# A hybrid two-layer model on one Trainium2 core: the first norm laid out in one order, other credits and costs for the background of the expert loops, and gate rows turned ahead of the last gates

## The chip, the cores and the metric

The kernel runs on one core of one Trainium2 chip. The metric is the device time of one execution in microseconds (us), and of several runs the median counts. All the matrix work goes through TensorE (PE in the profile); VectorE (DVE), ScalarE (ACT) and GpSimd (POOL) do the rest, each in the order in which its instructions were put, and SyncE (SP), ScalarE and GpSimd issue the DMA transfers.

## The reference

A sequence of 512 tokens with 1024 features goes through two layers. Each layer has a mixer and an expert network, each behind a norm whose shift, scale and gate come from one conditioning vector `c`:

```python
for layer in range(DEPTH):
    g, mw, mb = mix_norms[layer]
    shift, scale, gate = ada_modulation(c, mw, mb)      # silu(c) @ mw + mb, in three parts
    h = rms_norm(x, g) * (1.0 + scale) + shift
    mixer = rglru_mixer if layer % N_MIXERS == 0 else fox_mixer
    x = x + gate * mixer(h, *mixer_params[layer])
    g, mw, mb = ffn_norms[layer]
    shift, scale, gate = ada_modulation(c, mw, mb)
    h = rms_norm(x, g) * (1.0 + scale) + shift
    x = x + gate * peer_ffn(h, *peer_params[layer])
```

Layer 0 mixes by a gated linear recurrence (two input projections, a causal convolution of width 4, block-diagonal gates, a scan, gelu), layer 1 by attention with forget gates. The expert network picks for each token and each of 8 heads the 16 best of 16384 experts by two sets of keys, and adds up `gate * gelu(u . h) * v` over the 128 picks of a token.

## The kernel before

**Numbers.** Products are taken in three passes: every float32 operand is split into a rounded high part (`hi`, a copy on ScalarE) and the remainder (`lo`, a subtraction on DVE), and a product is hi·hi + hi·lo + lo·hi. So each weight block costs ScalarE a `whi` (L179) and DVE a `wlo` (L180) ahead of TensorE. `Stream` holds the plan of all weight blocks of the whole kernel in order; `fetch` issues a load on SP's queue, `fill` splits, `take` hands a block out.

**Order.** The program is written as straight Python and a list scheduler with a model of the machine lays out each engine's instructions. It may move an instruction ahead of another one that stands earlier in the program, unless both are given to `tc.keep_in_program_order` (here `pin`): pinned instructions of an engine keep the program's order among themselves. Within an engine the chip then executes strictly in the order laid out.

**The first norm** (`norm_first`, L252 to L348) is woven with the first modulation and the first four projections. The modulation columns of layer 0's mixer are dot products on DVE (`dot`, L300) of weight rows with silu(c); ScalarE makes a column of each (L302, L305). The token tiles are squared and scaled (L364 to L370), transposed into eight PSUM banks (L311), and for each of the eight feature blocks k `finish(k)` makes `hk` (L327), `hhi` (L328) and `hlo` (L329). Blocks of the first projection's weights are taken one step behind, and `products(k - 1)` runs the matmuls that are possible by then (L321 to L323). Of this only the dots and the `hlo` are pinned.

**The recurrent mixer** (`lru`) then takes chunk after chunk: projection, convolution, a second projection through gelu (L701), and behind each second chunk the gates of two chunks (L660 to L680). `Background` runs the modulation rows of what follows: `pump(credit)` adds credit and runs steps of generators as long as it is positive; each step yields its cost. `grow_fn` (`row_of`, L224) turns the eight gate columns into a row: a transpose on TensorE, a copy on ScalarE (L231), a small store on ScalarE's queue (L232) and a broadcast load on GpSimd's (L233). It stands between the last two groups of gates; the out-projection (L528 to L530) follows.

**The expert loop** (`peer`, L1147 and around) treats 384 of the 512 tokens densely: it goes over 128 chunks of 128 experts; a chunk's activations are either computed (24 matmuls, L486 to L488) or, for 56 of them, loaded back from where an earlier stage stored them (`at<-ascr`); they are multiplied by the gates (L1133), split (L1137, L1140) and multiplied with the chunk's `v` (18 matmuls, L1147). The last 128 tokens are done beside it by gathering rows of single experts (`gathered`, L1023 to L1064): 128 steps with `u` rows (L1044), then modulation rows (`mod_gen`, L196 to L221: a load on GpSimd's queue and a DVE product, L211), then 128 steps with `v` rows (L1059 for the first, L1061), then in layer 0 six more modulation rows. All use a ring of 8 buffers. Each step is put at 1.2 of credit, and `PUMPS` says how much credit a computed and a stored chunk give. What is left when the loop ends is run behind it by `bg.finish()`. Then the ring's room is given back, the tokens `x` are loaded into it by GpSimd (L123), and for each token tile from the last to the first DVE adds the gated result (L498, L499), ScalarE squares (L381), and DVE scales (L398) for the next norm, whose transposes (L425) follow on TensorE.

**The attention mixer** (`fox`) ends with the same `grow_fn`, behind its last output gates (L1367, L1368), ahead of `finish_mixer`, which splits `y` (`split`, L248 and L249) for the out-projection.

## Time and profile before

| what | us |
|---|---|
| median of 3 runs | 3088.3 (3087.58 to 3090.57) |
| the profiled execution, device time | 3089.21 |
| its span, first to last instruction | 3087.4 |
| granted TensorE clock, mean | 0.996 |

The profile shows one execution. In the rows of the timeline the columns are: start in us from the span's start, duration in us, engine (a `q` behind it marks the issue of a DMA), line of the kernel, operation, output<-inputs by the program's names, shapes, count of merged instructions, and in brackets the idle time of the engine just before and what ended it. In the grouped rows of the page stand, behind the count, the busy time in us, the mean of one in ns, and after the second bar the idle time of the engine ahead of these instructions. A row of the waits says who waited for whom: total in us, times, longest. A row by windows gives for a stretch its length and each engine's busy time (instructions) in the order PE, weight loads, DVE, ACT, POOL, then the granted TensorE clock, the share of the DMA engines' time and GB/s. Matmuls overlap, so the distance of their starts tells their rate, not their duration.

### The profile page before, as it was taken

How to read it: one execution, taken by the hardware profiler on the slowest of the kernel's cores; microseconds unless marked ns; L12 is line 12 of the kernel's file. 1: busy time of each engine (PE TensorE's matmuls, PEld its weight loads, DVE VectorE, ACT ScalarE, POOL GpSimd, SP SyncE). 2: the span in 40 equal slices, each digit the busy share in tenths (PEclk: the TensorE clock that was granted, in tenths of full speed). 3: DMA queues.
4: the chain of work that ended last, by engine and by line, in shares of the span. 5: the costliest groups of instructions: out<-in, count | busy, mean ns of one | idle time of the engine just before them, and what ended most of it. 6: DMA issues, size and time to landing. Idle time of an engine off the chain costs nothing.

```text
span 3087.4 us, 44585 instructions
## 1 busy us (share of the span) xinstructions
PE 3026.6 (98%) x16196; PEld 2676.5 (87%) x16196; DVE 2569.5 (83%) x5272; ACT 1480.4 (48%) x2183; POOL 953.1 (31%) x842
## 2 busy tenths in 40 slices
PE   7999999999999999999899999999999999999999
PEld 5778899998888888888777778899998888888888
DVE  7876989878888988898679967899868887888887
ACT  5764247873333333333458844267853333333332
POOL 0001430006554335554011003400025454445452
PEclk9999999999999999999999999999999999999999
DMA  7443245779999999999432123346799999999996
GB/s 275 169 163 141 97 153 197 265 292 390 381 361 374 366 352 372 373 347 341 164 121 77 63 103 128 121 157 245 271 333 377 335 357 349 355 328 354 355 326 242
DMA packets 295469, 815.85 MB, mean 264 GB/s; under 512 B 24624, under 2 KB 147536, under 8 KB 266704
## 3 DMA queue, kind: packets, MB, share of 16 engines
q1 hardware_dynamic: 164304, 388.77, 35.1%
q0 software_dynamic: 89408, 321.43, 27.9%
q10 hardware_dynamic: 41536, 102.80, 8.7%
q8 instruction: 127, 2.08, 0.3%
q14 instruction: 94, 0.77, 0.1%
HBM read 731.89 MB, written 81.02 MB: 263 GB/s over the span
## 4 chain that ended last, share of the span: by engine, by line
PE 71%; DVE 15%; issue 6%; ACT 4%; DMA 3%; POOL 1%; SPq 0%; DVEq 0%; POOLq 0%; ACTq 0%
PE vacc L1147 29%; PE pacc L486 11%; PE pacc L488 10%; PE pacc L487 10%; PE gps L991 3%; DVE wlo L180 2%; DVE ge L898 1%; DMA at<-ascr 1%; DVE tk L823 1%; PE oacc L529 1%; PE oacc L528 1%; PE oacc L530 1%; DVE mw L211 1%; ACT whi L179 1%; DVE idxs L822 1%
## 5 line engine op out<-in xcount | busy, mean ns | idle before, releaser
L179 ACT ACTIVATE whi<-wraw 128x1024 fp32r<-128x1024 f32 (+1 forms) x646 | 665.3, 1034 | 581.5 <-PE pacc L487 401.2
L486 PE MATMUL pacc<-hhi,whi 128*128 128x384 f32 (+1 forms) x2600 | 915.7, 352 | 1.2 <-ACT ge L701 1.2
L488 PE MATMUL pacc<-hhi,wlo 128*128 128x384 f32 (+1 forms) x2600 | 909.4, 350 | 5.5 <-DVE wlo L180 5.2
L487 PE MATMUL pacc<-hlo,whi 128*128 128x384 f32 (+1 forms) x2600 | 907.3, 349 | 0.0
L180 DVE TENSOR_TENSOR wlo<-wraw,whi 128x1024 fp32r<-128x1024 f32 (+1 forms) x584 | 705.8, 1212 | 202.6 <-ACT whi L179 199.8
L1147 PE MATMUL vacc<-wlo,wh 128*128 128x512 f32 x1536 | 600.2, 391 | 1.8 <-DVE wlo L180 1.8
L1147 PE MATMUL vacc<-whi,wl 128*128 128x512 f32 x1536 | 600.4, 391 | 0.0
L1147 PE MATMUL vacc<-whi,wh 128*128 128x512 f32 x1536 | 597.8, 389 | 0.0
L488 PEld LDWEIGHTS pacc<-hhi,wlo 128*128 128x128 f32 x2600 | 488.8, 188 | 31.5 <-DVE wlo L180 8.5
L486 PEld LDWEIGHTS pacc<-hhi,whi 128*128 128x128 f32 x2600 | 489.3, 188 | 27.7 <-ACT ge L701 1.6
L487 PEld LDWEIGHTS pacc<-hlo,whi 128*128 128x128 f32 x2600 | 489.3, 188 | 26.9
L1137 ACT ACTIVATE wh<-at 128x384 fp32r<-128x384 f32 x256 | 133.9, 526 | 740.1 <-DVE at L1133 356.9
L1031 POOL DMA_INDIRECT rows<-in_l_v_dram,ei x256 | 362.8, 1417 | 368.5 <-DVE accg L1061 332.1
L1031 POOL DMA_INDIRECT rows<-in_l_u_dram,ei x256 | 370.8, 1448 | 323.4 <-DVE rows L1044 267.8
L1147 PEld LDWEIGHTS vacc<-whi,wl 128*128 128x128 f32 x1536 | 288.3, 188 | 60.3
L1147 PEld LDWEIGHTS vacc<-wlo,wh 128*128 128x128 f32 x1536 | 288.3, 188 | 59.6 <-DVE wlo L180 2.2
L1147 PEld LDWEIGHTS vacc<-whi,wh 128*128 128x128 f32 x1536 | 288.5, 188 | 57.1
L1061 DVE SCALAR_TENSOR_TENSOR accg<-rows,act,accg 128x1024 f32<-128x1024 f32 x254 | 325.2, 1280 | 2.6 <-DMA rows<-in_l_v_dram,ei 2.2
L1044 DVE SCALAR_TENSOR_TENSOR rows<-rows,hn 128x1024 f32<-128x1024 f32 x256 | 304.7, 1221 | 0.0
L1133 DVE TENSOR_TENSOR at<-at,gtile 128x384 f32<-128x384 f32 x256 | 141.6, 555 | 135.0 <-DMA at<-ascr 127.4
L993 ACT ACTIVATE st<-gps 128x512 f32<-128x512 f32 x192 | 186.4, 1115 | 28.9 <-PE gps L991 28.4
L180 POOL TENSOR_TENSOR wlo<-wraw,whi 128x1024 fp32r<-128x1024 f32 (+1 forms) x62 | 125.3, 2032 | 185.3 <-ACT whi L179 185.3
(314 smaller groups left out, 3421.8 us busy)
## 6 DMA issues: line engine op xcount, KB each, us to landing
wraw<-in_l_uT_dram SPq DMA_DIRECT2D x128, 1024.0 KB, 5.7
wraw<-in_l_v_dram SPq DMA_DIRECT2D x128, 1024.0 KB, 9.3
gscr<-st ACTq DMA_DIRECT2D x48, 1024.0 KB, 4.9
gtile<-gscr SPq DMA_DIRECT2D x90, 512.0 KB, 12.8
mw<-in_l_ffn_mw_dram POOLq DMA_DIRECT2D x48, 512.0 KB, 4.7
ascr<-at ACTq DMA_DIRECT2D x112, 192.0 KB, 3.1
at<-ascr ACTq DMA_DIRECT2D x112, 192.0 KB, 6.9
mw<-in_l_mix_mw_dram POOLq DMA_DIRECT2D x32, 512.0 KB, 6.9
```

Of the source, the lines that this page charges most:

```text
L179: self.pin(nc.scalar.activation(hi, raw, AF.Copy))
L180: self.pin((nc.gpsimd if self.on_pool else nc.vector).tensor_sub(lo, raw, hi))
L486: nc.tensor.matmul(ps, whi[:, k, :], hhi[:, k, :n], start=(k == 0), stop=False)
L487: nc.tensor.matmul(ps, whi[:, k, :], hlo[:, k, :n], start=False, stop=False)
L488: nc.tensor.matmul(ps, wlo[:, k, :], hhi[:, k, :n], start=False, stop=(k == KD - 1))
L993: A.activation(st[:, :, q * 4:q * 4 + 4].rearrange("p e t -> p t e"), gps, AF.Copy, scale=1.0 / GSCALE)
L1031: i = nc.gpsimd.indirect_dma_start(out=rows, out_offset=None, in_=src, in_offset=bass.IndirectOffsetOnAxis(ap=ei[:, j:j + 1], axis=0))
L1044: V.scalar_tensor_tensor(r, r, 1.0, hn, op0=OP.mult, op1=OP.mult, accum_out=act[:, j:j + 1]))
L1061: tc.keep_in_program_order(V.scalar_tensor_tensor(acc, r, w, acc, op0=OP.mult, op1=OP.add))
L1133: pin(V.tensor_tensor(at.rearrange("p (b t) -> p b t", t=16), at.rearrange("p (b t) -> p b t", t=16), gts[c // 8][:, :, c % 8, :], op=OP.m ...
L1137: pin(A.activation(wh, at, AF.Copy))
L1147: T.matmul(acc[t][d], x[:, ts], y[:, d, :], start=(i == 0 and x is wh and y is vh), stop=(i == PK - 1 and x is wl))
```

## The change

Five edits:

1. In `norm_first` every ScalarE and DVE instruction of the columns, of `finish` and of the weight splits is pinned. Weight block k is split in step k (not k + 1): `whi` right behind `hhi`, `wlo` behind `hlo`, through a list `hold` in which the stream leaves the subtraction. `products(k)` follows in the same step. Blocks 4 and 5 are split behind the last step.
2. Behind the first column stands a gelu of a single column (128x1) into a spare tile, so that gelu's table is loaded there.
3. `PUMPS` go from (4.15, 1.3) to (4.45, 1.4) in layer 0 and from (3.75, 1.15) to (3.9, 1.2) in layer 1, and a modulation row in the expert loops counts 1.45 instead of 1.2.
4. The gate row is turned earlier: in `lru` in chunk 9 of 0 to 10, ahead of the last two groups of gates; in `fox` ahead of the last three gates.
5. The first step with a `v` row (L1059) is pinned like the others.

```diff
-PUMPS = ((4.15, 1.3), (3.75, 1.15))
+PUMPS = ((4.45, 1.4), (3.9, 1.2))
...
             self.pin(nc.scalar.activation(hi, raw, AF.Copy))
-            self.pin((nc.gpsimd if self.on_pool else nc.vector).tensor_sub(lo, raw, hi))
+            if self.hold is None:
+                self.pin((nc.gpsimd if self.on_pool else nc.vector).tensor_sub(lo, raw, hi))
+            else:
+                self.hold.append((lo, raw, hi))
...
-        yield 1.2
+        yield unit
...
+        pin = tc.keep_in_program_order
+
         def dot(r):
...
             if r < KD:
-                A.activation(cols[r], d, AF.Identity, bias=sub.b[:, r:r + 1])
+                pin(A.activation(cols[r], d, AF.Identity, bias=sub.b[:, r:r + 1]))
...
         dot(KD)
+        pin(A.activation(g.spare[:, 0:1], g.mhalf, AF.Gelu))
         for t in g.order:
...
+        def high(b):
+            g.stream.spare, g.stream.hold, g.stream.pin = nw if b < 2 else None, hold, pin
+            w.append(g.stream.take(0))
+            g.stream.spare, g.stream.hold, g.stream.pin = None, None, lambda x: x
...
-            A.activation(hk, xt[k], AF.Identity, scale=cols[KD + k], bias=cols[k])
-            A.activation(hhi[:, k, :], hk, AF.Copy)
-            return lambda: tc.keep_in_program_order(V.tensor_sub(hlo[:, k, :], hk, hhi[:, k, :]))
+            pin(A.activation(hk, xt[k], AF.Identity, scale=cols[KD + k], bias=cols[k]))
+            pin(A.activation(hhi[:, k, :], hk, AF.Copy))
+            return lambda: pin(V.tensor_sub(hlo[:, k, :], hk, hhi[:, k, :]))
 
         for k in range(KD):
             if k in (0, 2):
                 next(moved)
             low = finish(k)
+            if k < m:
+                high(k)
             if k + 1 < KD:
                 dot(KD + k + 1)
                 dot(k + 1)
             low()
-            if 1 <= k <= m:
-                g.stream.spare = nw if k <= 2 else None
-                w.append(g.stream.take(0))
-            if k == KD - 2:
+            if k < m:
+                pin(V.tensor_sub(*hold.pop(0)))
+            if k == KD - 1:
                 g.stream.fill(m + 1)
-            if k:
-                products(k - 1)
-        products(KD - 1)
+            products(k)
...
                         gates((j - 2, j - 1))
+                    if j == NR - 2:
+                        grow = grow_fn(psum)
                     bg.pump(LP)
                 bg.finish()
-                grow = grow_fn(psum)
                 gates((NR - 1,))
...
                 if j == 0:
-                    V.tensor_scalar(acc, r, w, None, op0=OP.mult)
+                    i = V.tensor_scalar(acc, r, w, None, op0=OP.mult)
                 else:
-                    tc.keep_in_program_order(V.scalar_tensor_tensor(acc, r, w, acc, op0=OP.mult, op1=OP.add))
+                    i = V.scalar_tensor_tensor(acc, r, w, acc, op0=OP.mult, op1=OP.add)
+                tc.keep_in_program_order(i)
...
                         bg.finish()
+                        if j == KD - 1:
+                            grow = grow_fn(psum)
                         n = (KD - LATE) // 2
                         for i in range(LATE + (j + 2 - KD) * n, LATE + (j + 3 - KD) * n):
                             gate(i)
-                grow = grow_fn(psum)
...
-            return mod_gen(g, pool, a[p + "_mw"], mods[p], rows, bufs, bufs < 8, queue, ring)
+            return mod_gen(g, pool, a[p + "_mw"], mods[p], rows, bufs, bufs < 8, queue, ring, 1.45 if ring else 1.2)
```

More of the change, by code (lines that the diff above doesn't have):

```diff
@@ L152, in __init__ @@
         self.spare = None
+        self.hold = None
         self.pin = lambda x: x
@@ L193, in take, with mod_gen @@
         return got
-def mod_gen(g, pool, mwT, sub, rows, bufs=2, pin=True, queue=None, ring=None):
+def mod_gen(g, pool, mwT, sub, rows, bufs=2, pin=True, queue=None, ring=None, unit=1.2):
     nc = g.nc
@@ L298, in dot @@
             d = nw.tile([128, 1], F32, name="dot", tag="dot", bufs=4)
-            tc.keep_in_program_order(
-                V.scalar_tensor_tensor(wf, wf, 1.0, g.sc, op0=OP.mult, op1=OP.mult, accum_out=d))
+            pin(V.scalar_tensor_tensor(wf, wf, 1.0, g.sc, op0=OP.mult, op1=OP.mult, accum_out=d))
             if r < KD:
-                A.activation(cols[r], d, AF.Identity, bias=sub.b[:, r:r + 1])
+                pin(A.activation(cols[r], d, AF.Identity, bias=sub.b[:, r:r + 1]))
             else:
                 k = r - KD
-                A.activation(cols[r], d, AF.Identity, scale=sub.g[:, k:k + 1], bias=bg[:, k:k + 1])
+                pin(A.activation(cols[r], d, AF.Identity, scale=sub.g[:, k:k + 1], bias=bg[:, k:k + 1]))
         dot(KD)
+        pin(A.activation(g.spare[:, 0:1], g.mhalf, AF.Gelu))
         for t in g.order:
@@ L313, in norm_first @@
                 dot(0)
-        w, ps = [], []
+        w, ps, hold = [], [], []
+        def high(b):
+            g.stream.spare, g.stream.hold, g.stream.pin = nw if b < 2 else None, hold, pin
+            w.append(g.stream.take(0))
+            g.stream.spare, g.stream.hold, g.stream.pin = None, None, lambda x: x
         def products(s):
```

## The prediction

> **What bounds the kernel now.** The page comes first, then TensorE's waits, then the timeline around each place where TensorE stands.
>
> ```profile
> span 3087.4 us, 44585 instructions
> ...
> PE 3026.6 (98%) x16196; PEld 2676.5 (87%) x16196; DVE 2569.5 (83%) x5272; ACT 1480.4 (48%) x2183; POOL 953.1 (31%) x842
> ...
> L179 ACT ACTIVATE whi<-wraw 128x1024 fp32r<-128x1024 f32 (+1 forms) x646 | 665.3, 1034 | 581.5 <-PE pacc L487 401.2
> ...
> L1061 DVE SCALAR_TENSOR_TENSOR accg<-rows,act,accg 128x1024 f32<-128x1024 f32 x254 | 325.2, 1280 | 2.6 <-DMA rows<-in_l_v_dram,ei 2.2
> L1044 DVE SCALAR_TENSOR_TENSOR rows<-rows,hn 128x1024 f32<-128x1024 f32 x256 | 304.7, 1221 | 0.0
> ```
>
> TensorE is busy for 3026.6 of 3087.4 us and the change takes no matmul away, so all it can win is 60.8 us of TensorE's idle time and whatever matmuls lose at a lower clock. No saving on another engine counts unless it ends in one of those gaps. Of TensorE's waits (total, times, longest) these belong to the change, beside the start's:
>
> ```profile
> PE pacc L488 <- DVE wlo L180: 5.2, 6, 2.0
> ...
> PE pacc L486 <- ACT ge L701: 1.2, 1, 1.2
> ...
> PE oacc L528 <- ACT grow L231: 0.9, 1, 0.9
> ```
>
> TensorE stands, or runs at a lower clock, at four places where the diff works: the first norm (11 to 56 us), the step from u rows to v rows in layer 0's expert loop (1122), the end of that loop (1489 to 1519), and the places where the gate row is turned (206, 1806). The last 100 us hold no gap that the change can reach: there TensorE works without a stop into the last adds.
>
> **The first norm.** The vector engine's timeline:
>
> ```profile
> 18.74 1.21 DVE L300 SCALAR_TENSOR_TENSOR mrow<-mrow,sc 128x1024 f32<-128x1024 f32 x1
> ...
> 23.87 1.23 DVE L180 TENSOR_TENSOR wlo<-wraw,whi 128x1024 fp32r<-128x1024 f32 x1 [2.17 <-ACT whi L179]
> 25.02 1.22 DVE L300 SCALAR_TENSOR_TENSOR mrow<-mrow,sc 128x1024 f32<-128x1024 f32 x1
> ...
> 27.31 0.69 DVE L329 TENSOR_TENSOR hlo<-hk,hhi 128x512 fp32r<-128x512 f32 x1
> 27.91 1.22 DVE L300 SCALAR_TENSOR_TENSOR mrow<-mrow,sc 128x1024 f32<-128x1024 f32 x1
> ...
> 29.05 1.22 DVE L180 TENSOR_TENSOR wlo<-wraw,whi 128x1024 fp32r<-128x1024 f32 x1
> ...
> 45.64 1.23 DVE L300 SCALAR_TENSOR_TENSOR mrow<-mrow,sc 128x1024 f32<-128x1024 f32 x1
> ...
> 49.66 2.36 DVE L180 TENSOR_TENSOR wlo<-wraw,whi 128x1024 fp32r<-128x1024 f32 x2 [2.19 <-ACT whi L179]
> 51.94 0.69 DVE L329 TENSOR_TENSOR hlo<-hk,hhi 128x512 fp32r<-128x512 f32 x1
> ```
>
> What to see: DVE stands 2.17 us ahead of the first wlo, which was scheduled before two dots that could have run, and at the end two wlo of later blocks (49.66, after 2.19 us of waiting) stand ahead of the last hlo. From start to start a dot takes 1.14 us (27.91 to 29.05), a wlo 1.15 (23.87 to 25.02), an hlo 0.60 (27.31 to 27.91). ScalarE at the end of the stage:
>
> ```profile
> 48.05 0.63 ACT L328 ACTIVATE hhi<-hk 128x512 fp32r<-128x512 f32 x1
> ...
> 53.45 0.60 ACT L689 ACTIVATE xp<-pacc 128x512 f32<-128x512 f32 x1 [2.87 <-PE pacc L323]
> 54.06 1.28 ACT L701 ACT_TABLE_LOAD   x1
> 55.36 0.60 ACT L701 ACTIVATE ge<-pacc 128x512 f32<-128x512 f32 x1
> ...
> 56.99 0.22 ACT L627 ACTIVATE az<-lm 128x11 f32<-128x11 f32 x1
> ```
>
> The pinned order is, for each k: hk, hhi and (k below 4) whi on ScalarE; two dots, hlo, wlo on DVE; blocks 4 and 5 only behind the last hlo. Nothing is left to wait for but the work: from the first dot's start to the last's there are 13 dots, 4 wlo and 6 hlo, 13x1.14 + 4x1.15 + 6x0.60 = 23.0 us. From the last dot's start to the end of the last hhi it is as now, 48.68 - 45.64 = 3.0, and the hlo is 0.7 more: 26.7 in all, against 52.63 - 18.74 = 33.9 now. That gains 7.2.
>
> The gelu load goes the other way. It is moved to just behind the first column:
>
> ```profile
> 8.30 0.61 ACT L364 ACTIVATE xn<-x 128x512 f32<-128x512 f32 x1
> ```
>
> This Square starts with no idle time before it, so x is there, and 1.28 + 0.22 = 1.5 us are put ahead of it. The whole chain of x tiles behind it (squares, root, transposes, first hk) is 1.5 later; a later arrival of x tiles 2 and 3 could hide part, so the bounds are 0 and 1.5, and I take 1.5. TensorE's wait of 1.2 us for ge, which stood behind the load of 54.06, goes. Against that, 96 matmuls now have to follow a faster DVE while part of them still runs at the low clock, and the order on ScalarE of whi 4 and 5 against the first xp is open: I take off 1.4. Sum: 7.2 - 1.5 + 1.2 - 1.4 = **5.5 us gained**, bounds 7.5 gained (x hides half the load, nothing taken off) and 1.5 lost (load paid, rest hidden). New waits: ScalarE now holds hk and the columns of the next k behind whi; blocks 2 and 3 wait for the second weight load, and if it lands late, DVE's hlo and every product behind it are late with it. The page ScalarE: Activation LUTs of the Trainium skill, What ACT_TABLE_LOAD costs, adds a drain of about 1.38 us to each switch of set; by it the stage would gain 4.1. The trace speaks against it: the activation ahead of the load ended at 54.05, the load began at 54.06 and ended at 55.34, and the next activation began at 55.36.
>
> **Gate rows.** In the first mixer the out-projection waits for the copy of the gate row, since it takes over that PSUM bank; in the second the copy and its DMA issue stand ahead of the first yhi, which TensorE awaits (rows of ScalarE's timeline; the wait of the first mixer is the 0.9 us of the fence above):
>
> ```profile
> 1804.91 0.25 ACT L231 ACTIVATE grow<-pacc 8x128 f32<-8x128 f32 x1
> ...
> 1805.53 4.28 ACT L248 ACTIVATE yhi<-y 128x512 fp32r<-128x512 f32 x8 [0.37 <-ACT grow L231]
> ```
>
> Turned ahead of the last gates, transposes, copy, ScalarE's DMA issue and POOL's broadcast lie under projections. **0.9 + (1805.53 - 1804.91) = 1.5 us gained**; bounds 0 and 1.5, since a bank of the projections' ring is taken for one copy, which TensorE could await once instead.
>
> **From u rows to v rows, layer 0.** The first v row's step was not pinned and got ahead of the last modulation rows, before its data:
>
> ```profile
> 1112.88 0.75 DVE L1059 TENSOR_SCALAR accg<-rows,act 128x1024 f32<-128x1024 f32 x1 [3.51 <-DMA rows<-in_l_v_dram,ei]
> ```
> ```profile
> 1122.90:1126.40 3.50, 3.50 (x13) 3.50 (x12) 3.50 (x9) 0.00 (x0) 2.26 (x2) 0.51 0.86 277
> ```
>
> DVE stood for 3.51 us, its lead on TensorE was used up, and at 1122 TensorE had the longest of its waits for wlo, 2.0; then it had half its clock for 3.5 us (0.51), worth 1.7. Pinned behind the six rows left, the step finds its data. **3.7 gained**, bounds 0 and 3.7. That the rows count 1.45 instead of 1.2 makes them fewer per chunk (4.45/1.45 = 3.1 for 4.15/1.2 = 3.5), which costs nothing: TensorE has no other wait there.
>
> **The end of layer 0's loop.** From the code: 66 chunks that are computed and 54 that are stored pump, so the credit was 66x4.15 + 54x1.3 = 344.1 against 256x1.2 + 38x1.2 = 352.8 of steps: eight steps remain for the flush behind the loop. Now it is 66x4.45 + 54x1.4 = 369.3 against 307.2 + 38x1.45 = 362.3: the steps end some three chunks before the loop does. (Layer 1: 309.6 against 316.8, now 322.2 against 318.8; but it ends in TensorE's own work, so nothing is won.) In the trace, DVE, POOL, TensorE:
>
> ```profile
> 1487.00 1.22 DVE L211 SCALAR_TENSOR_TENSOR mw<-mw,sc 128x1024 f32<-128x1024 f32 x1
> ...
> 1496.96 0.69 DVE L499 TENSOR_TENSOR x<-x,gt 128x512 f32<-128x512 f32 x1 [6.79 <-DMA x<-xs]
> ...
> 1503.56 0.68 DVE L498 TENSOR_TENSOR gt<-vacc,grow 128x512 f32<-128x512 f32 x1
> ...
> 1509.37 0.88 DVE L398 TENSOR_SCALAR xn<-x,rs 128x512 f32<-128x512 f32 x2
> ```
> ```profile
> 1487.60 1.57 POOL L123 DMA_DIRECT2D x<-xs  x3 [2.48 <-issue]
> ```
> ```profile
> 1489.42 0.50 PE L1147 MATMUL vacc<-wlo,wh 128*128 128x512 f32 x1 [1.76 <-DVE wlo L180]
> 1489.76 0.39 PE L1147 MATMUL vacc<-whi,wl 128*128 128x512 f32 x1
> 1489.99 0.40 PE L1147 MATMUL vacc<-whi,wh 128*128 128x512 f32 x1
> ...
> 1501.34 0.39 PE L1147 MATMUL vacc<-whi,wl 128*128 128x512 f32 x1
> ...
> 1512.97 0.79 PE L1263 MATMUL vacc<-whi,hhi 128*128 128x512 f32 x1 [1.09 <-DVE hhi L420]
> 1513.56 0.63 PE L1264 MATMUL vacc<-wlo,hhi 128*128 128x512 f32 x1
> 1513.98 0.63 PE L1263 MATMUL vacc<-whi,hhi 128*128 128x512 f32 x1
> ```
>
> The last modulation row ends at 1488.2; x is loaded into room that these rows give back, so POOL issues it at 1487.6, DVE gets it at 1496.96, and everything behind (adds, roots, transposes, first value product at 1512.97) hangs on that. The same rows push back a wlo: 1.76 us at 1489.42. With the steps done by then x is long there, and the accumulators decide. Expert products start 0.23 us apart (1489.76 to 1489.99), so the last ends at 1501.6; the accumulators of token tile 1 are full 24 matmuls earlier: 1501.6 - 24x0.23 - 1.8 (the wait gone) = 1494.3. From DVE's add of tile 1 (1503.56) to the last tile's scaling (1509.37) is 5.8 us, from there to the product 3.6: 1494.3 + 9.4 = 1503.7 for 1512.97, **9.3 gained**. The products run 0.42 us apart (1513.56 to 1513.98) instead of 0.23 until 1519; 14 x 0.19 = 2.7 us, of which I count half, **1.3**, because DVE's hhi, hlo and wlo come no faster. Bounds for the two: 1.8 (only the wlo) and 12.
>
> **The sum.** 5.5 + 1.5 + 3.7 + 9.3 + 1.3 = 21.3 us off the profiled execution's 3089.2 gives 3067.9; the median of the runs is 0.9 below that execution, so 3067.
>
> **The rivals.** *x stays late* (15%): another tenant of that room holds x back, or the scheduler leaves the rows where they are, so that the pump doesn't do what its numbers say. Only the 1.8 us of the wlo is won: 3067 + 8.8 = 3076. For it: the trace names POOL's last wait "issue", not the rows. *The start gives nothing* (13%): the load costs 1.5 and the products stay bound elsewhere: 3067 + 7 = 3074. *DMA as the bound* (5%):
>
> ```profile
> 690.00:1025.00 335.00, 335.00 (x1640) 297.99 (x1640) 285.45 (x432) 120.75 (x168) 182.83 (x129) 1.00 0.98 373
> ```
> The DMA engines are 98% taken. This stretch holds nearly all of the layer's 128 u rows (x256 over two layers) of 0.52 MB each; 7.2% more of them in the same time (4.45/4.15) are 4.8 MB, and were 373 GB/s the ceiling, that is 13 us there and as much in the v rows, less some 9 that the modulation rows give back: 3067 + 17 = 3084, no change. Against it: DVE waited 2.6 us for v rows in all and not at all for u rows. The Trainium skill, DMA: Bandwidth & Descriptors, Where 436 GB/s comes from, has HBM bind at about 358 GB/s for a core; by that rule this rival would hold, but the 373 of the row above is already over it. *Slower* (7%): DVE's idle time in the loops cannot be filled, since it works in order. Then every row step brought forward goes onto TensorE: half of 325.2 + 304.7 us by 7.2% in layer 0 and by 4% (3.9/3.75) in layer 1, 22.7 + 12.6 = 35 us: 3102. It decides once 11 us more (152 x 7.2%) no longer fit into the 49.5 us that DVE idles between 690 and 1025. Against it: ScalarE waits 401 us for TensorE to give weight buffers back, so that the supply runs ahead of TensorE, which stood for nothing in those 335 us.
>
> **How the numbers follow.** The forecast has 60%. About 0.2% (6 us) is what a measurement of this kernel tells from no change; all but the last two cases are more than 6 us faster. With a little for several rivals at once: faster 0.86, within 0.2% 0.08, slower 0.06. The range goes from 3061 (the upper bounds, 7.5 + 1.5 + 3.7 + 12 = 24.7 us, and the 3 us of waits for wlo that are left beside the one at 1122) to 3082 (the first two rivals together).
>
> **What would show it.** Right: gelu's table loaded near 8.5 us and none near 54; no wlo ahead of the last hlo, and that hlo ending near 47; no wait of DVE for the first v row; no modulation row behind the loop, x issued well before TensorE's last expert products, and the first value product some 2 us behind the last of them; no idle time on TensorE between 690 and 1025. Wrong: waits of TensorE for wlo, or of DVE for rows, inside the loops.

## The result, and the profile after

The changed kernel takes 3071.3 us (median of 6 runs, 3069.29 to 3075.46), the kernel before took 3088.7 beside it (6 runs, 3085.99 to 3096.03): ratio 0.9942, 95% interval 0.9929 to 0.9955. Run again later with 5 rounds the ratio was 0.9935 (0.9921 to 0.9948). The profiled execution of the changed kernel took 3075.46 us, the longest of its six; the profiled one of the later runs took 3070.92. Where the two differ, both are given below.

The head of the page after:

```profile
span 3073.7 us, 44567 instructions
...
PE 3021.1 (98%) x16196; PEld 2672.5 (87%) x16196; DVE 2567.1 (84%) x5272; ACT 1479.7 (48%) x2184; POOL 972.2 (32%) x842
...
L1072 DVE SCALAR_TENSOR_TENSOR accg<-rows,act,accg 128x1024 f32<-128x1024 f32 x254 | 324.5, 1278 | 0.4
L1055 DVE SCALAR_TENSOR_TENSOR rows<-rows,hn 128x1024 f32<-128x1024 f32 x256 | 304.0, 1218 | 0.0
```

The same work sits in a span 13.7 us shorter; DVE waits no more for rows than before (0.4 and 0.0 us). The stages, cut at TensorE's instructions (us, in the profiled executions of the kernel before, of the changed kernel, and of the changed kernel in the later runs; then the gain that the prediction gave and the two measured):

| stage | before | after | after, again | predicted | gained |
|---|---|---|---|---|---|
| start to first projection of the mixer | 56.01 | 50.21 | 50.16 | 5.5 | 5.8, 5.9 |
| recurrent mixer and out-projection | 212.80 | 214.67 | 214.48 | 0.9 | -1.9, -1.7 |
| expert network 0 up to its chunk 64 | 838.45 | 838.51 | 838.40 | 0 | -0.1, 0.1 |
| chunk 64 to 80 (u rows to v rows) | 103.08 | 99.25 | 100.15 | 3.7 | 3.8, 2.9 |
| chunk 80 to 123 | 268.77 | 270.41 | 268.46 | 0 | -1.6, 0.3 |
| chunk 123 to first value product | 33.85 | 24.26 | 24.26 | 9.3 | 9.6, 9.6 |
| attention mixer to its last product | 290.53 | 290.91 | 290.89 | 1.3 | -0.4, -0.4 |
| from there to its out-projection | 2.72 | 1.61 | 1.61 | 0.6 | 1.1, 1.1 |
| up to layer 1's expert loop | 473.54 | 474.55 | 473.56 | 0 | -1.0, 0.0 |
| layer 1's chunks 0 to 123 | 781.63 | 783.25 | 781.11 | 0 | -1.6, 0.5 |
| to the end | 26.06 | 26.07 | 26.06 | 0 | 0.0, 0.0 |

The start, in the timeline after (ScalarE, DVE, TensorE):

```profile
8.36 1.28 ACT L313 ACT_TABLE_LOAD   x1
9.66 0.20 ACT L313 ACTIVATE spare<-mhalf 128x1 f32<-128x1 f32 x1
...
12.21 0.62 ACT L374 ACTIVATE xn<-x 128x512 f32<-128x512 f32 x1
...
19.43 0.78 ACT L338 ACTIVATE hk<-pacc,col_l_mix,col_l_mix 128x512 f32<-128x512 f32 x1 [2.16 <-PE pacc L317]
...
49.04 0.60 ACT L711 ACTIVATE ge<-pacc 128x512 f32<-128x512 f32 x1
```
```profile
19.14 1.21 DVE L305 SCALAR_TENSOR_TENSOR mrow<-mrow,sc 128x1024 f32<-128x1024 f32 x1
...
45.24 0.69 DVE L340 TENSOR_TENSOR hlo<-hk,hhi 128x512 fp32r<-128x512 f32 x1 [1.23 <-ACT hhi L339]
46.19 2.36 DVE L182 TENSOR_TENSOR wlo<-wraw,whi 128x1024 fp32r<-128x1024 f32 x2 [0.26 <-ACT whi L180]
```

The table is loaded at 8.36 and not again ahead of ge at 49.04. The row at 12.21 is the fifth of the squares; it starts without waiting. The last hlo ends at 45.93 instead of 52.63, and the wlo of blocks 4 and 5 now stand behind it. The end of layer 0's loop (DVE, POOL, TensorE):

```profile
1445.51 1.22 DVE L215 SCALAR_TENSOR_TENSOR mw<-mw,sc 128x1024 f32<-128x1024 f32 x1
...
1480.28 0.69 DVE L509 TENSOR_TENSOR x<-x,gt 128x512 f32<-128x512 f32 x1
```
```profile
1438.09 1.57 POOL L123 DMA_DIRECT2D x<-xs  x3 [2.48 <-issue]
```
```profile
1493.22 0.39 PE L1159 MATMUL vacc<-whi,wl 128*128 128x512 f32 x1
1493.46 2.78 PE L435 MATMUL xa<-ident,xn 128*128 128x128 f32 x24
1497.31 0.50 PE L1275 MATMUL vacc<-whi,hhi 128*128 128x512 f32 x1 [1.07 <-DVE hhi L430]
```

The last modulation row ends at 1446.7, 46 us ahead of the last expert product (1493.22); x is issued at 1438.09 and DVE adds to it without waiting. TensorE goes from the last expert product straight into transposes.

The first step with a v row finds its data (DVE, no idle time ahead of it), and TensorE has no wait between 690 and 1110 us:

```profile
1112.22 0.75 DVE L1070 TENSOR_SCALAR accg<-rows,act 128x1024 f32<-128x1024 f32 x1
```

Two new stalls stand in the profiled execution after, one in each layer. DVE waits for a stored activation, the wlo behind it is late, and TensorE waits for that. Waits of TensorE for wlo inside the loops are a sign that the prediction named for being wrong; it came here, and what became of it is told with after_again.

```profile
1280.34 0.56 DVE L1145 TENSOR_TENSOR at<-at,gtile 128x384 f32<-128x384 f32 x1 [3.95 <-DMA at<-ascr]
...
2854.64 0.56 DVE L1145 TENSOR_TENSOR at<-at,gtile 128x384 f32<-128x384 f32 x1 [6.38 <-DMA at<-ascr]
```
```profile
1283.28 0.45 PE L498 MATMUL pacc<-hhi,wlo 128*128 128x384 f32 x1 [1.54 <-DVE wlo L182]
...
2857.58 0.45 PE L498 MATMUL pacc<-hhi,wlo 128*128 128x384 f32 x1 [1.38 <-DVE wlo L182]
```

### The profile page after: what moved, and what is told of

It reads as the page before. It is cut to its first block, busy times and chain, and to the rows that moved or that the text cites. A ratio compares the mean times of both kernels' runs of the same rounds, so it can differ in the third digit from the quotient of the medians.

```text
span 3073.7 us, 44567 instructions
## 1 busy us (share of the span) xinstructions
PE 3021.1 (98%) x16196; PEld 2672.5 (87%) x16196; DVE 2567.1 (84%) x5272; ACT 1479.7 (48%) x2184; POOL 972.2 (32%) x842
## 4 chain that ended last, share of the span: by engine, by line
PE 75%; DVE 13%; issue 5%; ACT 3%; DMA 3%; POOL 0%; DVEq 0%; SPq 0%; POOLq 0%; ACTq 0%
PE vacc L1159 31%; PE pacc L496 11%; PE pacc L498 11%; PE pacc L497 11%; PE gps L1002 3%; DMA at<-ascr 2%; DVE wlo L182 2%; DVE accg L1072 1%; PE oacc L539 1%; PE oacc L540 1%; PE oacc L538 1%; DVE ge L909 1%; DVE tk L834 1%; DVE idxs L833 1%; DVE idxs L836 1%
## 5 line engine op out<-in xcount | busy, mean ns | idle before, releaser
L182 DVE TENSOR_TENSOR wlo<-wraw,whi 128x1024 fp32r<-128x1024 f32 (+2 forms) x580 | 699.2, 1210 | 184.5 <-ACT whi L180 183.3
L1042 POOL DMA_INDIRECT rows<-in_l_u_dram,ei x256 | 383.3, 1497 | 280.5 <-DVE rows L1055 221.7
L1042 POOL DMA_INDIRECT rows<-in_l_v_dram,ei x256 | 369.0, 1441 | 322.0 <-DVE accg L1072 281.6
```

The source lines that it names most:

```text
L182: self.pin((nc.gpsimd if self.on_pool else nc.vector).tensor_sub(lo, raw, hi))
L1042: i = nc.gpsimd.indirect_dma_start(out=rows, out_offset=None, in_=src, in_offset=bass.IndirectOffsetOnAxis(ap=ei[:, j:j + 1], axis=0))
```

## The experiments

Twelve runs of eleven variants and of the changed kernel once more, 5 to 12 executions each, timed beside the kernel before. That one took 3088.7 us beside the changed kernel above and 3091.0 to 3091.5 beside the experiments, so the ratios compare better than the medians. Stage lengths below are those of the table above, cut in the experiment's own profiled execution.

| kernel | median us | ratio to before (95%) |
|---|---|---|
| norm_only | 3086.5 | 0.9981 (0.9972 to 0.9990) |
| pump_only | 3079.5 | 0.9962 (0.9948 to 0.9976) |
| pump_undone | 3082.3 | 0.9970 (0.9959 to 0.9982) |
| pump_pin_undone | 3085.2 | 0.9978 (0.9969 to 0.9987) |
| gelu_first | 3070.8 | 0.9930 (0.9916 to 0.9943) |
| grow_undone | 3076.0 | 0.9956 (0.9943 to 0.9969) |
| v0_unpinned | 3072.4 | 0.9940 (0.9927 to 0.9953) |
| unit_undone | 3071.2 | 0.9931 (0.9917 to 0.9944) |
| pump_more | 3084.3 | 0.9979 (0.9968 to 0.9989) |
| l1_old | 3077.2 | 0.9957 (0.9944 to 0.9970) |
| after_again | 3071.3 | 0.9935 (0.9921 to 0.9948) |
| best_43 | 3070.0 | 0.9926 (0.9913 to 0.9940) |

**Only the order of the first norm** (norm_only).

It is the kernel before with edit 1 whole (the pins, `hold`, blocks split one step earlier) and nothing else:

```diff
+            if k < m:
+                high(k)
...
-            if 1 <= k <= m:
-                g.stream.spare = nw if k <= 2 else None
-                w.append(g.stream.take(0))
...
+            products(k)
```

> Only the pinned order of the first norm, without the early gelu; all else as before the change. Theory A (DVE's order gave the gain, and the early table load cost the chain only 0.4 us of its 1.5): the first product comes at about 21.5 us (23.89 before, 21.87 with the whole change), the table load is back between the first xp and ge and TensorE's 1.2 us of waiting with it, so the first projection behind the loop starts at 56.01 - 5.8 - 0.4 + 1.2 = 51.0; the whole run 3088.7 - 5 = 3083.7, plus the 1 us or so that the recurrent mixer gives back. Theory B (the load put ahead of the squares costs its full 1.5 us): first product 20.4, first projection 56.01 - 5.8 - 1.5 + 1.2 = 49.9. Theory C (the gain came from moving the table load, not from the order): first projection at 55 or later, 3088.

The load is back ahead of the first ge (ScalarE, TensorE):

```profile
48.88 1.28 ACT L710 ACT_TABLE_LOAD   x1
50.17 0.60 ACT L710 ACTIVATE ge<-pacc 128x512 f32<-128x512 f32 x1
```
```profile
50.82 0.50 PE L495 MATMUL pacc<-hhi,whi 128*128 128x512 f32 x1 [0.54 <-ACT ge L710]
```

First projection at 50.82, as theory A had it (51.0). The arrival of the conditioning vector shifts the whole start by some tenths from run to run, so the fair length is from the first column to the first projection: 56.01 - 8.01 = 48.0 before, 50.82 - 8.72 = 42.1 here, 50.21 - 7.97 = 42.2 with the whole change. The order won 5.9 us, and the ratio of 0.9981 is as much. Where the table is loaded made 0.1, which is nothing that can be told: in the nine profiles that have the changed kernel's first norm this length runs from 41.3 to 42.2. Which part of edit 1 does it, the pins or the blocks split a step earlier, was not tried.

**The gelu ahead of the first column** (gelu_first).

```diff
-        dot(KD)
         pin(A.activation(g.spare[:, 0:1], g.mhalf, AF.Gelu))
+        dot(KD)
```

> The changed kernel with the gelu of one column put ahead of the first column, where ScalarE waits 2.19 us for the first dot, so that its table load of 1.28 us lies in that wait. Theory A (only 0.4 us of the load reaches the chain, since the root of the second token tile and the columns wait for DVE's dots): first square 1.5 us earlier, first transpose near 11.1, but first product only 0.4 earlier (21.5) and first projection 49.8; the time of the run unchanged within 1 us. Theory B (the load delays the whole chain): first product 20.4, first projection 48.7, 3069.8. Theory C (the columns' own table is loaded again behind gelu's): two table loads, first projection 1.3 us later than with the whole change.

```profile
5.53 1.28 ACT L312 ACT_TABLE_LOAD   x1
...
7.53 0.39 ACT L310 ACTIVATE col_l_mix<-dot,bg,gain_l_mix 128x1 f32<-128x1 f32 x1 [0.51 <-DVE mrow L305]
...
11.38 0.63 ACT L374 ACTIVATE xn<-x 128x512 f32<-128x512 f32 x1 [1.02 <-DMA x<-in_x_dram]
```

The load lies in a wait and no second one comes. The first transpose is 1.9 us earlier than after (10.62 to 12.56), the first product 1.0 (20.87 to 21.87), the first projection 0.7 (49.48), of which 0.4 is the earlier first column (7.53 to 7.97). Squares that are ready sooner meet an x tile that is not there (1.02 us). So of the 1.5 us put ahead of the squares at most 0.3 to 0.7 reached TensorE (0.3 is within the spread just named): theory A, and the prediction's full 1.5 was wrong.

**The credits alone** (pump_only).

It is the kernel before with edit 3 alone:

```diff
-PUMPS = ((4.15, 1.3), (3.75, 1.15))
+PUMPS = ((4.45, 1.4), (3.9, 1.2))
-        yield 1.2
+        yield 1.45 if ring else 1.2
```

> Only the new credits and the higher count of modulation rows; the first v row's step unpinned, the first norm and the gate rows as before. Theory A (rows flushed behind layer 0's loop held x back): no modulation row behind the loop, no wait of TensorE for wlo near the loop's end, the first value product some 4 us behind the last expert product instead of 11.6, together 9.6 us; the stall of 2 us and the half clock at the step from u to v rows (3.8 us) stay, since they come from the unpinned step; and the two new stalls for stored activations (1.6 in layer 0, 1.9 in layer 1) come with it, since the gathers are denser: 3088.7 - 9.6 + 3.5 = 3082.6. Theory B (the stalls for stored activations are chance or another edit's): no such stalls, 3079. Theory C (the credits, not the pin, removed the stall between u and v rows): 3.8 less than either. Theory D (another tenant of the room holds x back): the first value product still 11 us behind the last expert product, 3086 or more.

```profile
1104.12 0.75 DVE L1059 TENSOR_SCALAR accg<-rows,act 128x1024 f32<-128x1024 f32 x1
```

From chunk 123 to the first value product it took 24.26 us, all of the 9.6. The unpinned first v row no longer runs ahead of its data either (no wait in the row above), and chunk 64 to 80 takes 99.7: theory C for that stall. Of the new stalls for stored activations one came (1.3 us at 2671.66), at another place than after.

**The credits undone** (pump_undone), and **credits and pin undone** (pump_pin_undone).

Both are the changed kernel with

```diff
-PUMPS = ((4.45, 1.4), (3.9, 1.2))
+PUMPS = ((4.15, 1.3), (3.75, 1.15))
...
-            return mod_gen(g, pool, a[p + "_mw"], mods[p], rows, bufs, bufs < 8, queue, ring, 1.45 if ring else 1.2)
+            return mod_gen(g, pool, a[p + "_mw"], mods[p], rows, bufs, bufs < 8, queue, ring, 1.2)
```

and pump_pin_undone besides with the first v row's step as it was before (the diff of v0_unpinned, below).

> The changed kernel with the old credits and the old count of modulation rows; the first v row's step stays pinned. Theory A: the end of layer 0's loop is back as before the change (eight steps flushed behind it, wlo wait, first value product 11 to 12 us behind the last expert product), which costs 9.6; the stalls for stored activations at 1283 and 2858 go, which gives 3.5; the stall between u and v rows stays away: 3071.3 + 9.6 - 3.5 = 3077.4. Theory B (those stalls don't come from the credits): 3081. Theory C (the credits removed the stall between u and v rows): it is back and 3.8 more. Theory D (x is held back by another tenant): no loss, 3071 or less.

> The changed kernel with the old credits, the old count and the first v row's step unpinned: only the first norm, the early gelu and the gate rows are left of the change. Theory A (with the old credits the pin costs layer 1 what it wins in layer 0, since it sets the first v row back there too and with it the last): TensorE's stall between u and v rows in layer 0 is back (2 us, with the half clock 3.8), its wait for wlo 17 us before the end of layer 1's loop (4.1 us) is gone, and the time is that of the kernel with the old credits and the pin, ratio 0.997. Theory B (the wait in layer 1 has nothing to do with the pin): both are there, 0.998.

In pump_undone, with the pin kept, chunk 64 to 80 takes 99.25, so the pin too removes that stall by itself. Chunk 123 to the value product takes 33.67 again, but not by the way that the prediction named (POOL, DVE, TensorE of pump_undone):

```profile
1474.88 1.56 POOL L123 DMA_DIRECT2D x<-xs  x3 [2.48 <-issue]
```
```profile
1481.98 0.69 DVE L509 TENSOR_TENSOR x<-x,gt 128x512 f32<-128x512 f32 x1 [0.25 <-DMA x<-xs]
...
1493.42 0.17 DVE L1293 MEMSET sel<- 128x134 f32 x1 [4.97 <-PE vacc L1159]
```
```profile
1480.99 0.51 PE L1159 MATMUL vacc<-wlo,wh 128*128 128x512 f32 x1 [2.28 <-DVE wlo L182]
...
1494.52 0.39 PE L1159 MATMUL vacc<-whi,wl 128*128 128x512 f32 x1
...
1502.93 0.80 PE L1275 MATMUL vacc<-whi,hhi 128*128 128x512 f32 x1 [1.10 <-DVE hhi L430]
...
3058.94 0.52 PE L1159 MATMUL vacc<-wlo,wh 128*128 128x512 f32 x1 [2.20 <-DVE wlo L182]
```

Here x was in time (0.25 us of waiting). Two of the flushed rows stood ahead of a wlo of the last blocks on DVE (2.28 us of TensorE's at 1480.99, and a clock of 0.69 over the 3.4 us behind it); the last expert product comes 25.3 us behind chunk 123's first instead of 20.2. DVE then stands for 4.97 us until 1493.42 for the accumulators of tile 1, which are full some 1 us before the last product instead of 24 products (5.5 us), and the value product comes 8.4 us behind the last one instead of 4.1. 5.1 + 4.3 = 9.4. In pump_pin_undone x was 4.25 us late, and the stage took 34.01 us, almost the same.

In layer 1 the pin with the old credits costs time. The wait at 3058.94 stretches the part behind chunk 123 to 30.20 us; without the pin (pump_pin_undone) there is no such wait, and it takes 26.09, as before. These are single profiles; the times of the two kernels (0.9970 and 0.9978) can't be told apart. There the first v row starts 2.6 us behind chunk 60's first product instead of 16.9, and the last v row ends 7.1 us behind chunk 123's instead of 10.5. In exchange the stall between u and v rows is back in layer 0 (1.57 us at 1118.84; 101.07 for that stage). Theory A of both by their signs. The time of pump_undone is 5 us above what it gave, and layer 1's wait, which no theory had, is 4.1 of that.

**The first v row unpinned** (v0_unpinned).

```diff
-                    i = V.tensor_scalar(acc, r, w, None, op0=OP.mult)
+                    V.tensor_scalar(acc, r, w, None, op0=OP.mult)
                 else:
-                    i = V.scalar_tensor_tensor(acc, r, w, acc, op0=OP.mult, op1=OP.add)
-                tc.keep_in_program_order(i)
+                    tc.keep_in_program_order(V.scalar_tensor_tensor(acc, r, w, acc, op0=OP.mult, op1=OP.add))
```

> The changed kernel with the first v row's step unpinned again. The new credits alone removed TensorE's 2 us stall between u and v rows, and the pin alone did too. Theory A (each is enough, the pin adds nothing to the credits): no wait of DVE for the first v row, no stall of TensorE near 1115, 3071. Theory B (they remove it by different ways that only add up together, or the one run with the credits alone was chance): DVE waits 3 us or more, TensorE stalls 2 us, with the half clock 3.8: 3075.

DVE has no wait for the first v row (1100.99), TensorE waits 0.8 us near 1119; ratio 0.9940. Theory A: with the new credits the pin does nothing that can be measured. This profile has stalls of 1.6 and 0.7 us at 761 and 853 in the u rows, where the changed kernel, of the same order there, had none in two executions. In layer 1 it waits 1.8 us at 2669.29, at the chunk (63) where pump_only, the other kernel with the new credits and no pin, waits 1.3.

**The count of a modulation row undone** (unit_undone).

```diff
-            return mod_gen(g, pool, a[p + "_mw"], mods[p], rows, bufs, bufs < 8, queue, ring, 1.45 if ring else 1.2)
+            return mod_gen(g, pool, a[p + "_mw"], mods[p], rows, bufs, bufs < 8, queue, ring, 1.2)
```

> The changed kernel with modulation rows at 1.2 of credit again, the new credits kept. Theory A (the count of a modulation row does nothing that can be measured, as the prediction took it): no new stall between u and v rows, the steps end a little earlier, ratio 0.994. Theory B (20% denser modulation rows hold up the wlo): stalls of TensorE for wlo between 1015 and 1110, 2 to 4 us, ratio 0.995.

Ratio 0.9931, no stall between 1015 and 1110: theory A. The first v row starts at 1094.5 instead of 1112.2, which changes nothing. One wait of 1.7 us for a wlo stands at 1308.62.

**The gate rows undone** (grow_undone).

```diff
-                    if j == NR - 2:
-                        grow = grow_fn(psum)
...
+                grow = grow_fn(psum)
                 gates((NR - 1,))
```

(and the same for the attention mixer)

> The changed kernel with both gate rows turned at the old places. Theory A (only the attention mixer won): from TensorE's last product of the attention to the first of the out-projection 2.7 us again instead of 1.6, so 1.1 more; in the recurrent mixer the wait of 0.9 us for the copy is back, but the time from the first projection to the first product behind the mixer stays within the 213.0 to 215.5 us that it took with the early row: 3072.4. Theory B (both won, 0.9 and 1.1): 3073.3. Theory C (the early row costs the recurrent mixer more than the wait, since it takes a bank of the projections' ring): that stretch 1 us shorter, 212.8 as before the change, 3071.

```profile
197.53 1.28 ACT L682 ACT_TABLE_LOAD   x1
...
199.88 0.25 ACT L235 ACTIVATE grow<-pacc 8x128 f32<-8x128 f32 x1
```
```profile
200.19 0.50 PE L538 MATMUL oacc<-whi,yhi 128*128 128x512 f32 x1 [3.15 <-ACT grow L235]
```

The attention mixer loses its 1.1 us (2.72 against 1.61 us, the same in every kernel with the late and with the early row). The recurrent mixer loses more than any theory said, 217.4 us for the stage: the copy stands behind the chain of the gates and a table load, and TensorE waits 3.15 us for it, not 0.94 as before. Why so long is not shown; norm_only starts as early and waits 0.93. And this execution ran at half clock for 3.4 us twice there (from 101.7 and from 200.7), which is worth some 3.4 us of the stage. So it is not settled what the early row is worth there: without a half clock in the stage it took 212.8 to 214.7 us in seven profiles with the early row (214.5 and 214.7 in the changed kernel), and 212.8, 213.9 and 213.5 with the late one (before, pump_only, norm_only). TensorE's waits for grow turned into waits for others (xh and xl of the gates' inputs, whi and wlo of the out-projection).

**Still more credit** (pump_more), a step of 0.5 in layer 0 where the change's was 0.3.

```diff
-PUMPS = ((4.45, 1.4), (3.9, 1.2))
+PUMPS = ((4.95, 1.55), (4.3, 1.35))
```

> The changed kernel with still more credit: 4.95 and 1.55 in layer 0, 4.3 and 1.35 in layer 1, again as large a step as the change made. Theory A (DVE has room; the stalls for stored activations in the profile of the changed kernel are chance): nothing more to win and nothing lost, TensorE without stalls from 690 to 1490, DVE's total wait for stored activations between 119 and 156 us as in the six profiles so far, 3071. Theory B (denser gathers make the stored activations late): that total above 165 us, more stalls like the 1.6 and 1.9 of the changed kernel, 3075 or more. Theory C (DVE's idle time does not hold them): waits of TensorE for wlo in the u rows as well, 3080 or more. Theory D (DMA is the bound): DVE waits for rows.

Windows over the u rows, kernel before, changed kernel, pump_more (columns: length; PE, weight loads, DVE, ACT, POOL; clock, DMA share, GB/s):

```profile
690.00:985.00 295.00, 295.00 (x1442) 262.10 (x1442) 252.32 (x383) 107.36 (x149) 163.65 (x115) 1.00 0.99 376
```
```profile
690.00:985.00 295.00, 295.00 (x1439) 261.64 (x1438) 261.66 (x400) 105.28 (x146) 184.61 (x122) 1.00 1.02 388
```
```profile
690.00:985.00 295.00, 291.44 (x1421) 258.19 (x1420) 270.61 (x417) 104.88 (x146) 195.79 (x134) 1.00 1.03 402
```

and in the same stretch the waits of ScalarE for weights (before, after, pump_more) and, in pump_more up to 1110, those of TensorE:

```profile
ACT whi L179 <- DMA wraw<-in_l_v_dram: 5.0, 1, 5.0
```
```profile
ACT whi L180 <- DMA wraw<-in_l_v_dram: 20.2, 3, 8.0
```
```profile
ACT whi L180 <- DMA wraw<-in_l_v_dram: 28.0, 4, 10.1
...
ACT whi L180 <- DMA wraw<-in_l_uT_dram: 6.3, 3, 5.0
```
```profile
PE pacc L498 <- DVE wlo L182: 6.5, 5, 1.9
```

Theory C: the time is 11 to 14 us above the changed kernel's by the ratios. In the profile the stretch up to chunk 64 takes 847.4 us against 838.5, with five waits of TensorE for wlo. (Another 3.2 us lie in the recurrent mixer, which no credit of the loops touches; it ran at half clock for 6.8 us from 229.9 in this execution.) DVE's idle time in the 295 us falls from 42.7 (before) over 33.3 to 24.4 us, and the weights land later and later. Theory B falls: DVE waits less for stored activations (84 us in all against 138), since it comes to them later. The DMA engines moved 402 GB/s, so 376 was no ceiling. What speaks for them as part of the limit is that they are taken to 99% of the time already before, and that ScalarE's waits for weights in this stretch grow with the dose: 3.7 to 5.0 us in the four profiles at 4.15, 5.5 at 4.3, 9.3 to 29.3 in the eight at 4.45, 34.3 here. What speaks for DVE is its shrinking idle time. These runs don't tell the two apart.

**Layer 1's credits undone** (l1_old).

```diff
-PUMPS = ((4.45, 1.4), (3.9, 1.2))
+PUMPS = ((4.45, 1.4), (3.75, 1.15))
```

> The changed kernel with layer 1's credits back at 3.75 and 1.15. Theory A (layer 1 ends in TensorE's own work, so rows that are late there cost nothing, as the prediction had it): 3071, and no stall behind 3040. Theory B (the last v rows stand ahead of a wlo, as in the kernel with all the old credits): a wait of TensorE for wlo of 2.4 us some 15 us before the end of the loop and 1.8 more at the low clock, 3075.5.

```profile
3057.55 0.50 PE L1159 MATMUL vacc<-wlo,wh 128*128 128x512 f32 x1 [2.34 <-DVE wlo L182]
...
3061.20 0.79 PE L1159 MATMUL vacc<-wlo,wh 128*128 128x512 f32 x1 [1.13 <-DVE wlo L182]
```

Theory B, and more: two waits, and 33.05 us behind chunk 123 instead of 26.06, 7.0 lost in this profile; by the ratios the time is 5 to 7 us above the changed kernel's. By the count, rows at 1.45 leave more to flush here than rows at 1.2 (318.8 of steps against 309.6 of credit, with 1.2 it was 316.8); what that adds to the pin's 4.1 was not tried by itself.

**The changed kernel again** (after_again), and **a weaker dose with the early gelu** (best_43).

The latter is gelu_first with the modulation rows at 1.2, as in unit_undone, and

```diff
-PUMPS = ((4.45, 1.4), (3.9, 1.2))
+PUMPS = ((4.3, 1.35), (3.9, 1.2))
```

> The changed kernel once more, beside the three others on the same chip. Theory A (its stalls for stored activations, 1.6 and 1.9 us, were chance of that execution): they don't come at the same places, ratio 0.994 to the kernel before. Theory B (they belong to the change): stalls of more than 1.4 us of TensorE near 1283 and 2858 again.

> The changed kernel with the gelu ahead of the first column, credits of 4.3 and 1.35 in layer 0 (3.9 and 1.2 in layer 1 as changed), and modulation rows at 1.2 again. By the sum of credits, 66x4.3 + 54x1.35 = 356.7 against 352.8, the rows still end ahead of layer 0's loop, but the u rows are 3.4% less dense than with 4.45. Theory A (4.45 stands at the edge of what DVE and the DMA engines can take): the first value product still 24.3 us behind the first product of chunk 123, ScalarE's waits for weight loads between 690 and 985 below the 20 us of the changed kernel, no stall of TensorE between 690 and 1060, ratio 0.992 to 0.993. Theory B (the rows end too close to the loop's end): x is late, the first value product 26 us or more behind chunk 123, ratio 0.996. Theory C (no edge at 4.45): nothing told apart from the kernel with the early gelu alone, 0.993.

In after_again the stalls at 1283 and 2858 are not there, as theory A has it. But chance decides only whether they come and how long they last; the place is not all chance. The one at 1283 stands at chunk 93, and there TensorE waits in five of the eight profiles at 4.45 (0.4 to 1.9 us; after 1.54, l1_old 1.88), in none of the four at 4.15 and not in best_43. That speaks for the denser gathers as a cause, as theory A of pump_only had it, and against chance alone; it is not more than that. In best_43:

```profile
1494.80 0.50 PE L1275 MATMUL vacc<-whi,hhi 128*128 128x512 f32 x1 [1.07 <-DVE hhi L430]
```
```profile
ACT whi L180 <- DMA wraw<-in_l_v_dram: 5.5, 1, 5.5
```

24.26 us behind chunk 123, ScalarE's waits for weights back at 5.5 us, no wait of TensorE above 0.6 us between chunk 0 and 123 of both layers. Theory A's signs are there; but 0.9926 (0.9913 to 0.9940) can't be told from 0.9935 and 0.9942 of the changed kernel. All of the gain at the loop's end is had with half the added credit.

## Why the prediction was right, point by point

**First norm, 5.5 predicted, 5.8 measured.** From the first dot's start to the end of the last hlo it gave 26.7 us; it is 45.93 - 19.14 = 26.8, against 33.9. Sized wrong were terms that offset each other: the load costs the chain 0.4 us instead of 1.5 (first hk at 19.43, 19.02 before), because ScalarE had a wait for an x tile there at its fifth square, which now starts 0.16 us later (12.21; ScalarE of the kernel before below): the bound that the prediction named and did not take. And TensorE needs 50.21 - 45.93 = 4.3 us from the last hlo to the first projection, 2.1 more than the 3.4 - 1.2 before, where 1.4 was taken off. 7.1 - 0.4 + 1.2 - 2.1 = 5.8. (The upper bound given as 7.5 adds up to 7.65, 7.2 - 0.75 + 1.2.) So the 5.8 near 5.5 owes something to luck. By the prediction's estimate with the drain that the Trainium skill, ScalarE: Activation LUTs, What ACT_TABLE_LOAD costs, adds to a switch, 4.1 would have been left. The trace agrees with its 1283 ns for the load and not with the drain: load from 8.36 to 9.64, gelu at 9.66.

```profile
12.05 0.63 ACT L364 ACTIVATE xn<-x 128x512 f32<-128x512 f32 x1 [1.20 <-DMA x<-in_x_dram]
```

**Gate rows, 1.5 predicted, 1.1 shown.** The attention mixer won 1.1 where 0.6 was taken: the row left ScalarE, and the transpose on TensorE went with it. TensorE's first out-product there, before and after:

```profile
1806.21 0.50 PE L528 MATMUL oacc<-whi,yhi 128*128 128x512 f32 x1 [2.06 <-ACT yhi L248]
```
```profile
1789.83 0.50 PE L538 MATMUL oacc<-whi,yhi 128*128 128x512 f32 x1 [1.33 <-ACT yhi L252]
```

In the recurrent mixer the wait of 0.9 is gone and the stage is 1.7 to 1.9 us longer; the step that failed is that a wait removed there ends the stage sooner. TensorE meets other late operands of ScalarE and DVE. That the edit lengthens the stage is not shown: kernels with the same row there differ by as much (grow_undone).

**From u to v rows, 3.7 predicted, 2.9 and 3.8 measured**; the cause given was one of two. Pinning the step does it (pump_undone) and the new credits do it (pump_only); with either, the other has nothing left to do here. And 1.7 of the 3.7 hung on the half clock that one execution had: norm_only has a wait of 1.8 us at the same place, keeps its clock and takes 101.3 us for the stage, not 103.1. Its window behind that wait (clock 1.00, where the prediction's row had 0.51):

```profile
1117.60:1121.10 3.50, 3.50 (x20) 3.50 (x21) 3.50 (x8) 0.00 (x0) 2.16 (x3) 1.00 0.98 360
```

**End of layer 0's loop, 9.3 predicted, 9.6 measured**, in every kernel with 4.3 of credit or more: 24.25 to 24.26 us in ten profiles against 33.7 to 35.6 in the four at 4.15. The sum held; that the value product comes "some 2 us" behind the last expert product did not: it is 4.1, as the sum itself implied (1503.7 against 1501.6 - 1.8). That x held back was all of it is too simple: with x in time but the rows still behind the loop (pump_undone) late wlo and late accumulators cost the same. Both come from the flushed rows, and the credits remove both. The 1.3 for the half clock was 2.6 at the 24th value product, 0.5 at the 33rd, and none of it is left at the mixer's end. Of the operands that the prediction feared, hhi costs the same before and after (1.7 us in two waits); new are waits for ScalarE's whi, which it did not name, and for DVE's wlo:

```profile
1504.16 0.73 PE L1275 MATMUL vacc<-whi,hhi 128*128 128x512 f32 x2 [0.98 <-ACT whi L180]
...
1505.42 0.50 PE L1276 MATMUL vacc<-wlo,hhi 128*128 128x512 f32 x1 [0.53 <-DVE wlo L182]
```

**Layer 1.** "Nothing is won" was right for the sum, 26.06 and 26.07 us. But layer 1's end is not out of reach of the edits, as the prediction took it to be: with the old credits the pin costs 4.1 us there, with pin and higher count it is 7.0 (l1_old), and the credits of 3.9 pay for both (one profile each).

**The rivals.** *x stays late* fell (x is there at 1480). *The start gives nothing* fell (norm_only). *Slower* and *DMA as the bound* did not come at 4.45, but the limit they speak of is near: at 4.95 the gain in layer 0's loop is eaten. The first 9 us more (DVE's idle time from 42.7 to 33.3 us in the 295) cost the changed kernel's TensorE nothing there; the next 9 (33.3 to 24.4) made it wait, though 24 were left, so the point from which that rival decides was put too far off. The 358 GB/s that the prediction cited bound nothing (388 in the changed kernel's row above); the Trainium skill, HBM Reference, Specifications (TRN2), says of a core streaming alone about 425 GB/s, and pump_more's u rows come near it, with 419 GB/s from 950 to 970 us and a mean of 402.

**The sum.** 21.3 was predicted, 18.3 came in after_again and 13.7 in the first profile (span against span). Of the missing 3.0 against the former, 2.6 are the recurrent mixer, 0.8 the step from u to v rows, 1.7 the value products; 0.3 each came back in the first norm and at the loop's end, 0.5 from the gate row, 0.9 in the loops. By the medians it is 17.4 of 21.3. norm_only and pump_only by themselves give 0.0019 and 0.0038, together 0.0057 of the 0.0058 to 0.0065 of the whole change. The first profile lacks another 4.5, mainly 2.0 and 2.1 us in the two stretches with the stalls and 1.0 in layer 1's routing, less 0.9 between chunks 64 and 80.

## What to carry to other kernels

Work that runs beside a loop must end inside it: eight rows flushed behind the loop cost TensorE 9.6 us here. That is not their own time on DVE, which ran beside TensorE's products (the last row ended at 1488.2, the last expert product began at 1501.3); they stand ahead of the last operands and in the room of the next stage's input. Raise the credit until that flush is gone and no further: 4.3 with rows at 1.2 did it as well as 4.45, and 4.95 lost 11 to 14 us. And before a removed wait is counted, ask which other operand of that stage arrives next: in the recurrent mixer no gain can be shown.

## What the runs showed of the hardware

**The clock behind a wait.** Behind each of TensorE's five waits of 2.2 to 2.4 us in the expert loops the clock fell (0.54 to 0.69 over the next 3.4 us; 0.54 in pump_undone at 3059, 0.57 in l1_old at 3057.6). Behind the eleven waits of 1.3 to 1.8 us there it stayed at 1.00, and in between it went either way: 1.87 us in pump_more at 859 kept 1.00, 1.88 us in l1_old at 1282.8 had 0.55. Outside the loops a wait of 2.0 us kept 1.00 (unit_undone at 101.5), and one of 1.84 had 0.54 (pump_more at 229.6, with a second wait of 0.7 behind it). In the routing even 1.2 us were enough in 7 of 28 cases; this is one of them, with the 3.4 us behind it:

```profile
1915.22 0.33 PE L876 MATMUL sps<-whi,ql 128*128 128x128 f32 x1 [1.22 <-DVE ql L253]
```
```profile
1915.22:1918.62 3.40, 3.40 (x18) 3.40 (x19) 3.37 (x23) 0.42 (x1) 3.25 (x8) 0.69 0.23 73
```

The three profiles with it in layer 1 (after, v0_unpinned, l1_old) took 474.5 us for the stretch up to the expert loop, the other eleven 473.5 to 473.6. So length alone doesn't decide, and a profile's price for a wait near 2 us is 2 us or 4. The Trainium skill, TensorE: Matmul & The Clock Gate, Part 1, describes a free-running window of 3413 ns; the length of the slow stretches agrees (0.50 from 1916.52 to 1919.93 here, 3.41 us). A window that falls on the waits by chance would also explain that equal waits differ, though no run shows where it begins. But waits well below a whole window were enough here.

**Spread of stalls.** With the credits at 4.45 the profiles have 0 to 2 stalls of 1.3 to 1.9 us within the loops (3 at 4.95), ahead of most of them a late load of stored activations (4.1 us of DVE's waiting in unit_undone at 1305.67); with those at 4.15 there is none but the one from u to v rows (chunk 67) and those at the loops' ends. Places recur, chunk 93 of both layers and chunk 63 of layer 1 among them, but not in every execution. One profile can so be 4.5 us off another of the same kernel.
